# The value projection of a stick-breaking attention as seven block products instead of eight

## The chip, the core and the metric

The kernel runs on one core of one Trainium2 chip. The metric is device time in microseconds for one execution of the whole program. All matrix products are made in three passes of a 32-bit format with a reduced mantissa: each operand is split into a high part and a low part (what is left), and high x high, high x low and low x high are summed. The engines are TensorE (PE: matmuls; PEld: its weight loads), VectorE (DVE), ScalarE (ACT), GpSimd (POOL) and the queue of SyncE (SP) that issues nearly all DMAs.

## The reference

Two layers on 512 tokens of width 1024: a pooling mixer with an MLP, then an attention with an MLP. Cut to what matters here:

```python
def stick_breaking_attention(q, k, v):            # 16 heads of 64, blocks of 128 queries
    z = einsum('bhqd,bhkd->bhqk', q_blk, k_blk) / 8
    log1m = where(mask, -softplus(z), 0.0)        # mask: key strictly before query
    excl = cumsum(log1m, reverse=True) - log1m
    a = where(mask, exp(log_sigmoid(z) + excl), 0.0)
    out = einsum('bhqk,bhkd->bhqd', a, v_blk)

def sq_relu_mlp(h, w_up, w_down):
    return matmul(square(relu(matmul(h, w_up))), w_down)

# layer 0: x += norm(pool_mixer(norm(x)));  x += norm(mlp(norm(x)))
kv = matmul(rms_norm(x, kv_norm_g), w_kv)         # (512 x 1024) @ (1024 x 2048): keys and values
# layer 1: q = norm(x) @ w_q;  x += norm(attention(q, k, v) @ w_o);  x += norm(mlp(norm(x)))
```

The value projection is the second half of that product: 512 x 1024 tokens by 1024 x 1024 weights.

## The kernel before

**Planner.** The program is written as a sequence of tile operations. A planner then fixes the order on each engine ahead of time: what stands first in the program goes first among the operations that it holds to be ready. Inside regions marked `manual_schedule` TensorE keeps the written order, and `issue_after(x)` keeps an operation behind `x` on its engine. A tile with `bufs=n` has n buffers under its tag, and the next use waits until one is released.

**First MLP (`mlp(0, ...)`, about 35 to 350 us of the span).** The up projection makes 32 blocks of 128 hidden units (`up` and `up_block`, L672 to 674). The down projection takes 28 of them in five groups through the class `Seven`, which already multiplies 2x2 blocks by seven products (L560), with combinations on VectorE (L514, L533), splits on ScalarE and VectorE (L272, L273) and sums into `y` on VectorE (L569). The last four hidden blocks go through `contract` plainly (`dn` weights, L310 to 312).

In 27 of the 35 steps of this MLP `split_apart` prepares weights of the attention beside it: load 512 KB, scale by the norm's gain on ScalarE (L144; eight calls on 128 columns for keys and queries, four on 256 for values), cast the high part on ScalarE (L219), subtract on VectorE (L220), and store both parts to device memory (`kept`, L175). All 24 of the attention's value, key and query weights go this way.

**Weights in time.** `queue` lists the weights in the order in which they will be used. `get` takes one; `fill` fetches ahead until four (`ahead`) are made and not yet used. `make` reloads a kept weight as two DMAs (L230). A weight that is not kept goes through `weight()`: load into `raw` (two buffers, L123), scale on ScalarE, cast on ScalarE (L133), subtract on VectorE (L135). Both ways need a buffer of `place`: three under the tag `w` and one under `wx`, so four weights in all. At the seam to the attention the first four entries of the attention's queue stand ahead of the MLP's last `dn` weights.

**Attention.** The order of work is `ATT_ORDER`, a list of short words:

- V: `values(u, tiles)`, four heads' values for some token tiles; 24 matmuls of 256 columns a tile (`mm3`, L310 to 312), copied out on ScalarE (L910).
- K: the first half of a key block (tokens 0 and 1). J: keys of a head pair. Q: its queries. Each is 24 matmuls of 512 columns or the same in halves (L672 to 674); ScalarE casts (L944, L945, L960) and VectorE subtracts (L946, L961).
- N: transpose a token tile into `xnh`, `xnl` (L383; split at L272, L273).
- S: the scores of a pair (L994), then for both heads sigmoids (L1019, L1023), a scan (L1025) and a product (L1029).
- T: transpose one head's weights (L1042), copied out by ScalarE (L1044). A: mix the values (L1053).
- O: a part of the output projection. E: its last part, with the norms.
- W: `split_here`, one step of preparing the eight output weights and four up weights of the second MLP. Each step stores one, splits one (L185, L186) and loads one (L194), into a buffer of `grow`, `spare` or, for two of four, `raw`.

The program runs all operations of a pair in that order: S of one pair, then J and Q of the next, then T and A of the first. With `V0` the value work stands spread over the pairs, a few token tiles at a time. The token tiles 2 and 3 come out of the first MLP's closing norms only after the attention has begun (N2, N3).

Of the kernel before, what the change touches and what calls it, by code (L numbers as in the profile page):

```python
# [55 lines left out]
    (w[0], int(w[1:2] or 0), [int(c) for c in w[2:]])  # L56
    for w in """V00 W K0 V01 N2 V02 N3 V03 J0 Q0 W V10 V11 S0 W J1 Q1 T00 T01 V13 S1 V12 A0 J2 W T10 W Q2 W W T11 A1
    S2 O00 O03 O01 J3 T21 Q3 O02 T20 S3 J4 A2 Q4 W V20 T30 S4 V21 W W J5 T31 Q5 A3 T40 W V23 T41
    V22 S5 A4 W J6 Q6 T51 T50 V30 S6 A5 J7 Q7 T60 T61 V31 S7 W W V33 V32 A6 O10 O11 T70 T71
    O12 A7 O13 E2""".split()  # L60
]


# [8 lines left out]
def trunk(ctx, tc, x, consts, gcol, grow, pw, wup, wdn, wq, wk, wv, wo, out):  # L72
# [80 lines left out]
    def place(k):  # L153
# [3 lines left out]
        if k == ("o", 6):  # L157
            both = att_pool[0].tile([P, 2, D], F32R, tag="v", bufs=2, name=name("w"))
# [18 lines left out]
    def split_here():  # L177
# [9 lines left out]
        if here:  # L187
# [7 lines left out]
            going.append([k, 0, raw, None])  # L195

    def split_apart(mp):
        if going and going[0][1] == 3:
            k, _, raw, hi, _ = going.pop(0)
            keep_parts(k, hi, raw)  # L200
        if apart:
            k, src, scaled = apart.pop(0)
            n = len(apart) % 5
            if n < 3:
                raw = mp.tile([P, D], F32, tag="apart", bufs=3, name=name("apart"))
            else:
                raw = spare_tile() if n == 3 else work.tile([P, D], F32, tag="grow", name=name("apart"))

            with tc.issue_after(latest["sp"].ins) if "sp" in latest else nullcontext():
                nc.sync.dma_start(raw, src)  # L210
            going.append([k, 0, raw, None, scaled])
        for x in going:
            k, n, raw, hi, scaled = x
            if n == 1:
                if scaled is not None:
                    scaled(raw)
            elif n == 2:
                hi = x[3] = apart_hi[0][:, len(kept) % 2]
# [27 lines left out]
    for l in range(2):  # L246
        if l == 1:
            n = len(queue)
            for what, i, part in ATT_ORDER:
                if what == "V" and 0 in part:  # L250
                    for h in range(2):
                        want(("v", i, h), wv[i, h], gains(C_KV * KC + 4 * h, 4))
                elif what == "J":
# [317 lines left out]
    def mlp(l, mp, update):  # L571
# [56 lines left out]
        for g, group in enumerate(groups):  # L628
# [6 lines left out]
            for i in range(7):  # L635
# [12 lines left out]
                else:  # L648
# [4 lines left out]
                    elif i == 5:  # L653
                        piece = lambda tag, k, bufs=1: mp.tile([P, k, D], F32R, tag=tag, bufs=bufs, name=name("dn"))
                        w, e, x = piece("w1", 3), piece("e", 1), piece("w", 3, 2)
                        c, d = (piece("apart", 1, 3)[:, 0] for _ in range(2))
                        dn_pool[0] = [[w[:, 0], w[:, 1]], [w[:, 2], e[:, 0]], [c, d], [x[:, 0], x[:, 1]]]
# [235 lines left out]
    with tc.tile_pool(name="att", bufs=1, reuse_waits="tile") as ap:  # L893
        att_pool[0] = ap

        def values(u, part):
            if u not in vs:
                w = [get(("v", u, h)) for h in range(2)]
                vs[u] = w, ap.tile([P, T, 4, HD], F32, tag="v", bufs=2, name=name("v"))
            w, v = vs[u]  # L900
            for s in part:
                need(s)
                pv = ps()
                for k in range(KC):
                    c = slice((k % 4) * 256, (k % 4) * 256 + 256)
                    mm3(
                        pv[:, :256], xnh[:, k, TS[s]], xnl[:, k, TS[s]],
                        in_turn(w[k // 4][0][:, c], 256), in_turn(w[k // 4][1][:, c], 256), k == 0, k == KC - 1,
                    )
                nc.scalar.copy(v[:, s].rearrange("p h d -> p (h d)"), pv[:, :256])  # L910

# [120 lines left out]
        def transposed(w):  # L1032
            parts = {}
            for tiles in ((0,), (1, 3), (2,)):
                pt = ps()
                c = 0
                turned = ap.tile([P, S], F32, tag="at", bufs=8, name=name("at"))
                for s in tiles:
# [8 lines left out]
        def mix_pair(p):  # L1047
            po, v = ps(), vs[p // 2][1]
            with tc.manual_schedule(engines={mybir.EngineType.PE}):
                for s in range(T):  # L1050
                    for a in range(2):
                        turned, c = parts[p, a][s]
                        nc.tensor.matmul(  # L1053
                            po[half[a], s * P :], v[:, s, (2 * p + a) % 4], turned[:, c : c + S - s * P],
                            start=s == 0, stop=s == T - 1, skip_group_check=True,
                        )
            if p < PAIRS - 1:
                both = ap.tile([P, D], F32R, tag="ohl", bufs=5, name=name("ohl"))
            else:
# [3 lines left out]

        vs, os, wos, y = {}, {}, {}, y_tiles()

# [11 lines left out]
        for what, i, part in ATT_ORDER:  # L1077
            if what == "V":
                values(i, part)
            elif what == "W":  # L1080
# [95 lines left out]
```

## Time and profile before

| | |
|---|---|
| median of 3 runs | 909.21 us (908.27 to 909.58) |
| the profiled execution | 909.54 us |
| its span in the profile | 907.7 us |
| granted TensorE clock | 0.998 |
| PE busy | 896.7 us (99%), 4762 matmuls |
| DVE busy | 663.4 us (73%) |
| ACT busy | 553.4 us (61%) |
| POOL busy | 92.0 us (10%) |
| DMA | 169.35 MB, mean 187 GB/s |

The profile is one execution. Its stage rows give busy time of each engine in a stretch of the span. The busy time of one matmul overlaps that of the next, so the distance between starts is what a matmul takes in a stream. Rows that group instructions read: line, engine, operation, output from input, shape, count, busy us, mean ns, then the idle time just before and what ended it.

### The profile page before, as it was taken

To read this page: it belongs to the slowest core of one execution; us is meant where nothing else is said; L and a number is where in the kernel's file an instruction comes from. 1 tells how busy PE (TensorE), PEld (TensorE's weight loads), DVE (VectorE), ACT (ScalarE), POOL (GpSimd) and SP (SyncE) were. 2 spreads that over 40 slices of the span, in tenths; PEclk is the share of its full clock that TensorE was granted. 3 is DMA by queue.
4 is the path that set the end of the run, shared out by engine and by line. 5 is a ranking of instruction groups with operands and counts; after the bars stand their busy time and mean duration, and the time that the engine had idled before them with its cause. 6 is when DMAs were issued, how large, how long until landed. Compare 5 with 4: busy or idle time off the path is not lost.

```text
span 907.7 us, 12363 instructions
## 1 busy us (share of the span) xinstructions
PE 896.7 (99%) x4762; PEld 783.4 (86%) x4762; DVE 663.4 (73%) x682; ACT 553.4 (61%) x956; POOL 92.0 (10%) x86
## 2 busy tenths in 40 slices
PE   9999999999999999999999999999999999999996
PEld 7998888888888888987888887898888888888886
DVE  5966798997988966476463664965596876968956
ACT  6668989797884638576656652456554454544632
POOL 2100000000000014000000000402130310303103
PEclk9999999999999999999999999999999999999999
DMA  7444989698693423999624355332504233133102
GB/s 286 144 185 137 350 295 336 265 327 334 220 352 142 162 93 117 365 414 333 238 110 168 149 196 184 139 129 86 205 23 164 92 139 117 46 140 116 47 24 92
DMA packets 46928, 169.35 MB, mean 187 GB/s; under 512 B 4832, under 2 KB 5306, under 8 KB 46870
## 3 DMA queue, kind: packets, MB, share of 16 engines
q1 hardware_dynamic: 46722, 168.55, 50.7%
q8 instruction: 37, 0.61, 0.3%
q14 instruction: 21, 0.17, 0.1%
q10 hardware_dynamic: 148, 0.02, 0.0%
HBM read 128.71 MB, written 39.85 MB: 186 GB/s over the span
## 4 chain that ended last, share of the span: by engine, by line
PE 91%; DMA 2%; DVE 2%; ACT 2%; issue 1%; POOL 1%; SPq 0%; POOLq 0%; DVEq 0%; ACTq 0%
PE ps L560 27%; PE ps L672 14%; PE ps L674 14%; PE ps L673 14%; PE ps L310 4%; PE ps L311 4%; PE ps L312 4%; PE ps L1053 2%; PE ps L1042 2%; PE ps L994 2%; PE ps L811 2%; DMA kept<-xn 1%; DMA xn<-in_wdn 1%; PE ps L787 1%; DVE x L357 1%
## 5 line engine op out<-in xcount | busy, mean ns | idle before, releaser
L560 PE MATMUL ps<-w,a 128*128 128x512 f32 x1176 | 267.1, 379 | 0.2 <-DVE a L273 0.2
L673 PE MATMUL ps<-xnl,w 128*128 128x512 f32 (+1 forms) x712 | 254.8, 358 | 0.6 <-DVE xnl L273 0.6
L672 PE MATMUL ps<-xnh,w 128*128 128x512 f32 (+1 forms) x712 | 254.9, 360 | 0.0
L674 PE MATMUL ps<-xnh,w 128*128 128x512 f32 (+1 forms) x712 | 254.7, 358 | 0.0
L560 PEld LDWEIGHTS ps<-w,a 128*128 128x128 f32 x1176 | 222.0, 189 | 32.4 <-DVE a L273 0.6
L673 PEld LDWEIGHTS ps<-xnl,w 128*128 128x128 f32 x712 | 135.0, 190 | 15.9 <-DVE xnl L273 1.0
L674 PEld LDWEIGHTS ps<-xnh,w 128*128 128x128 f32 x712 | 134.9, 190 | 16.0 <-issue 0.8
L672 PEld LDWEIGHTS ps<-xnh,w 128*128 128x128 f32 x712 | 134.3, 190 | 15.8 <-issue 0.5
L135 DVE TENSOR_TENSOR w<-raw,w 128x1024 fp32r<-128x1024 f32 x56 | 70.9, 1268 | 51.3 <-ACT w L133 51.3
L569 DVE TENSOR_TENSOR y<-ps,y 128x512 f32<-128x512 f32 x124 | 83.4, 683 | 26.2 <-PE ps L560 26.2
L133 ACT CAST w<-raw 128x1024 fp32r<-128x1024 f32 x56 | 58.4, 1044 | 69.1 <-PE ps L674 68.3
L345 POOL TENSOR_TENSOR y<-y,grow 128x512 f32<-128x512 f32 x12 | 18.8, 1568 | 550.3 <-ACT xn L276 550.3
L1025 DVE TENSOR_TENSOR_SCAN e<-u,begin 128x1280 f32<-128x1280 f32 x16 | 45.2, 2825 | 34.7 <-ACT u L1019 33.8
L272 ACT CAST w<-e 128x1536 fp32r<-128x1536 f32 (+1 forms) x30 | 41.7, 1390 | 40.3 <-DVE e L533 31.0
L272 ACT CAST a<-r 128x768 fp32r<-128x768 f32 (+1 forms) x60 | 47.0, 785 | 29.2 <-DVE r L514 17.7
L273 DVE TENSOR_TENSOR w<-e,w 128x1536 fp32r<-128x1536 f32 (+1 forms) x30 | 54.8, 1825 | 9.1 <-ACT w L272 8.9
L273 DVE TENSOR_TENSOR a<-r,a 128x768 fp32r<-128x768 f32 (+1 forms) x60 | 59.1, 985 | 0.0
L144 ACT ACTIVATE apart<-apart,gc 128x128 f32<-128x128 f32 (+1 forms) x136 | 43.7, 401 | 0.1
L273 DVE TENSOR_TENSOR w<-xn,w 128x1536 fp32r<-128x1536 f32 (+1 forms) x20 | 33.0, 1652 | 11.0 <-ACT w L272 10.6
L273 DVE TENSOR_TENSOR w<-w,w 128x1536 fp32r<-128x1536 f32 (+1 forms) x20 | 34.6, 1728 | 8.1 <-ACT w L272 8.1
L276 ACT ACTIVATE xn<-y 128x512 f32<-128x512 f32 (+1 forms) x24 | 14.9, 622 | 41.4 <-DVE y L418 41.4
L272 ACT CAST w<-xn 128x1536 fp32r<-128x1536 f32 (+1 forms) x20 | 27.8, 1390 | 19.4 <-PE ps L560 19.4
(145 smaller groups left out, 1345.2 us busy)
## 6 DMA issues: line engine op xcount, KB each, us to landing
w<-kept SPq DMA_DIRECT2D x70, 512.0 KB, 4.9
raw<-in_wup SPq DMA_DIRECT2D x62, 512.0 KB, 4.2
w<-in_wdn SPq DMA_DIRECT2D x8, 1536.0 KB, 6.7
kept<-wx SPq DMA_DIRECT2D x24, 512.0 KB, 6.2
xn<-in_wdn SPq DMA_DIRECT2D x8, 1536.0 KB, 6.6
kept<-apart SPq DMA_DIRECT2D x22, 512.0 KB, 4.9
kept<-xn SPq DMA_DIRECT2D x12, 512.0 KB, 8.1
kept<-spare SPq DMA_DIRECT2D x8, 512.0 KB, 5.5
```

The lines of the kernel that those rows point to most:

```text
L133: nc.scalar.copy(hi, raw)
L135: nc.vector.tensor_tensor(out=lo, in0=raw, in1=hi.bitcast(F32), op=ALU.subtract)
L144: nc.scalar.mul(c, c, gc[:, lo + k : lo + k + 1])
L272: latest["act"] = nc.scalar.copy(hi, src)
L273: latest["dve"] = nc.vector.tensor_tensor(out=lo, in0=src, in1=hi.bitcast(F32), op=ALU.subtract)
L310: nc.tensor.matmul(dst, ah, bh, start=start, stop=False)
L560: nc.tensor.matmul(bank, a[:, x, q, TS[t]], by_twos(w[:, z, q], NS[0]), start=start and q == 0 and k == 0, stop=q == self.n - 1 and k == 2 ...
L569: nc.vector.tensor_tensor(out=part, in0=bank, in1=part, op=ALU.add)
L672: nc.tensor.matmul(pu[:, cols], wh[:, k, :], xh, start=k == 0, stop=False)
L673: nc.tensor.matmul(pu[:, cols], wh[:, k, :], xl, start=False, stop=False)
L674: nc.tensor.matmul(pu[:, cols], wl[:, k, :], xh, start=False, stop=k == KC - 1)
L1025: nc.vector.tensor_tensor_scan(out=e[:, ::-1], data0=u[:, 1:][:, ::-1], data1=begin[:, ::-1], initial=0.0, op0=ALU.mult, op1=ALU.max,)
```

## The change

The value projection is made as C = X W with X and W cut into 2x2 blocks: two halves of the tokens (256 each) by two halves of the width, and two halves of the width by two halves of the heads. Seven products of such blocks replace eight. Each product is two token tiles by 512 columns: 4 x 3 matmuls of 512 columns a tile.

- Three products use weight blocks as they are (W11, W21, W22; `VALUES` 0, 5 and 6). They are no longer kept: `weight()` makes them in the attention, with two scalings each a half.
- Four use combined weight blocks. `value_forms` makes them in the first MLP in 27 steps: it loads and scales the four blocks of each half, combines them with four VectorE operations, splits and stores the results.
- From step 16 on, `split_apart` prepares keys and queries of pairs 0 to 3. Those of pairs 4 to 7 are no longer prepared there; `weight()` makes them in the attention.
- Four products use combined token blocks. `form` (F) makes the combinations on VectorE from the high and low parts and splits them.
- `value_product` (V) runs a product; products 0, 2, 4 and 6 add into the same two PSUM banks one after the other. Each result is copied by ScalarE or added by VectorE into `v_all`, which holds all heads.
- All seven products stand before pair 2 in the new `ATT_ORDER`. The W steps begin after A0, two to a pair.
- Buffers: `at` has 6 instead of 8, `ohl` 6 instead of 5; the tile of output weight 6 lies on the scan's operands.

```diff
 ATT_ORDER
-    V00 W K0 V01 N2 V02 N3 V03 J0 Q0 W V10 V11 S0 W J1 Q1 T00 T01 V13 S1 V12 A0 J2 W T10 W Q2 W W T11 A1
-    S2 O00 O03 O01 J3 T21 Q3 O02 T20 S3 J4 A2 Q4 W V20 T30 S4 V21 W W J5 T31 Q5 A3 T40 W V23 T41
-    V22 S5 A4 W J6 Q6 T51 T50 V30 S6 A5 J7 Q7 T60 T61 V31 S7 W W V33 V32 A6 O10 O11 T70 T71
-    O12 A7 O13 E2
+    V5 K0 N2 N3 F3 V3 J0 Q0 F2 S0 V1 J1 Q1 F1 V0 T00 T01 V2 F4 V4 S1 V6 A0 W J2 W Q2 T10 T11 S2 A1 W W J3 Q3
+    T20 T21 O00 S3 O01 A2 W W J4 O02 Q4 O03 T30 T31 S4 A3 W W J5 Q5 T40 T41 S5 A4 W W J6 Q6 T50 T51 S6 A5 W W J7 Q7
+    T60 T61 S7 W W A6 O10 O11 O12 T70 T71 O13 A7 E2
+VALUES = (
+    (0, "11", (0, 0)), (1, "s3", None), (2, "s2", None), (3, "22", None), (4, "s1", None),
+    (5, "12", (1, 0)), (6, "s4", (1, 1)),
+)
+    def value_forms():            # per half h, one entry a step, from step 8 * h on
+            listed = [
+                [(load, "B"), (load, "D")],
+                [(scale, "B"), (scale, "D"), (load, "A")],
+                [(make_form, "E", "D", "B", minus), (scale, "A")],
+                [(make_form, "B", "B", "A", minus)],
+                [(parts_of, "B"), (load, "C")],
+                [(store, "B", 4), (make_form, "G", "E", "A", plus), (scale, "C")],
+                [(parts_of, "E")],
+                [(store, "E", 1), (make_form, "C", "C", "G", minus)],
+                [(parts_of, "G")],
+                [(store, "G", 2), (parts_of, "C")],
+                [(store, "C", 3)],
+            ]
 def split_apart(mp):
-        if apart:
+        for job, *rest in form_steps[n]:
+            job(*rest)
+        if apart and n >= 16:
...
-            apart.extend(x for x in queue[n:] if x[0][0] != "o")
+            apart.extend(x for x in queue[n:] if x[0][0] in "kq" and x[0][1] < 4)
...
+        def form(i):
+            if i == 3:
+                s, z = sums[3], other = quarter(), quarter()
+                on(out=s, in0=high["11"], in1=high["21"], op=ALU.subtract)
+                on(out=z, in0=low["11"], in1=low["21"], op=ALU.subtract)
+                on(out=s, in0=s, in1=z, op=ALU.add)
+            elif i == 2:          # five such operations: 21 + 22, then minus 11
+            elif i == 1:
+                s = sums[1]
+            else:                 # two operations: 12 minus the sum of F2
+            hi, lo = (quarter().bitcast(F32R) for _ in range(2))
+            split(s, hi, lo)
+        def value_product(i):
+            key = VALUES[i][1]
+            w = [get(("v", i, h)) for h in range(2)]
+            for t in range(2):
...
+                for q in range(4):
+                    cols = NS[q % 2]
+                    for n, (x, z) in enumerate(((0, 0), (0, 1), (1, 0))):
+                        nc.tensor.matmul(
+                            bank, a[x][q], in_turn(w[q // 2][z][:, cols], 512),
+                            start=(i == 0 or not linked) and q == 0 and n == 0, stop=q == 3 and n == 2,
+                        )
+                if i == 1:
+                    to(1, 1, False)
+                    to(1, 0, True)
+                else:
+                    to(*{0: (0, 0, True), 2: (1, 0, True), 3: (1, 0, False), 4: (1, 1, True),
+                         5: (0, 0, False), 6: (0, 1, False)}[i])
+            fill()
```

More of the change, by code (lines that the diff above doesn't have):

```diff
@@ L157, in place @@
         if k == ("o", 6):
-            both = att_pool[0].tile([P, 2, D], F32R, tag="v", bufs=2, name=name("w"))
+            return [
+                att_pool[0].tile([P, NSEG + 1 + 55 * a], F32R, tag=f"u{a}", name=name("w"))[:, :D] for a in range(2)
+            ]
         elif k == ("o", 7):
@@ L195, in split_here, with load, scale, make_form @@
             going.append([k, 0, raw, None])
-    def split_apart(mp):
+    def value_forms():
+        steps = [[] for _ in range(27)]
+        for h in range(2):
+            names = "B0 D3 A1 E2 C4 G3".split() if h == 0 else "B0 D1 A2 E3 C4 G1".split()
+            spot = {x[0]: int(x[1]) for x in names}
+            source = {"A": (0, 0), "B": (0, 1), "C": (1, 0), "D": (1, 1)}
+            got = {}
+            def load(x, h=h, got=got, spot=spot):
+                t = got[x] = buffer(spot[x])
+                with tc.issue_after(latest["sp"].ins) if "sp" in latest else nullcontext():
+                    nc.sync.dma_start(t, wv[source[x]][h])
+            def scale(x, h=h, got=got):
+                gains(C_KV * KC + 4 * source[x][0] + 2 * h, 2)(got[x])
+            def make_form(out, x, y, op, got=got, spot=spot):
+                if out not in got:
+                    got[out] = buffer(spot[out])
+                nc.vector.tensor_tensor(out=got[out], in0=got[x], in1=got[y], op=op)
+            def parts_of(x, got=got):
+                hi = apart_hi[0][:, len(kept) % 2]
+                raw = got[x]
+                nc.scalar.copy(hi, raw)
+                nc.vector.tensor_tensor(out=raw, in0=raw, in1=hi.bitcast(F32), op=ALU.subtract)
+                got[x] = raw, hi
+            def store(x, i, h=h, got=got):
+                raw, hi = got[x]
+                keep_parts(("v", i, h), hi, raw)
+            minus, plus = ALU.subtract, ALU.add
+            listed = [
[10 more added lines that the diff above has]
+                [(store, "C", 3)],
+            ]
+            for n, jobs in enumerate(listed):
+                steps[8 * h + n].extend(jobs)
+        return steps
@@ new lines, in buffer @@
+    def buffer(n):
+        if n < 3:
+            return apart_raw[0][:, n]
+        return spare_tile() if n == 3 else work.tile([P, D], F32, tag="grow", name=name("apart"))
+    form_steps, apart_raw = [], [None]
+    def split_apart(mp):
+        if not form_steps:
+            form_steps.extend(value_forms())
+            apart_raw[0] = mp.tile([P, 3, D], F32, tag="apart", name=name("apart"))
+        n = split_apart.n = getattr(split_apart, "n", -1) + 1
+        for job, *rest in form_steps[n]:
+            job(*rest)
@@ L200, in split_apart @@
             keep_parts(k, hi, raw)
-        if apart:
+        if apart and n >= 16:
             k, src, scaled = apart.pop(0)
[L203 to L209, printed above, removed]
+            raw = buffer((0, 2, 1, 3, 4)[(n - 16) % 5])
+            with tc.issue_after(latest["sp"].ins):
                 nc.sync.dma_start(raw, src)
@@ L212, in split_apart @@
         for x in going:
[L213 to L217, printed above, removed]
+            k, m, raw, hi, scaled = x
+            if m == 1:
+                scaled(raw)
+            elif m == 2:
                 hi = x[3] = apart_hi[0][:, len(kept) % 2]
@@ L655, in mlp @@
                         w, e, x = piece("w1", 3), piece("e", 1), piece("w", 3, 2)
-                        c, d = (piece("apart", 1, 3)[:, 0] for _ in range(2))
+                        both = piece("apart", 3)
+                        c, d = both[:, 0], both[:, 1]
                         dn_pool[0] = [[w[:, 0], w[:, 1]], [w[:, 2], e[:, 0]], [c, d], [x[:, 0], x[:, 1]]]
@@ L894, in trunk @@
         att_pool[0] = ap
[L896 to L910, printed above, removed]
+        v_all = ap.tile([P, T, HEADS, HD], F32, tag="v", name="v")
@@ L1047, in mix_pair @@
         def mix_pair(p):
[L1048 removed]
+            po = ps()
             with tc.manual_schedule(engines={mybir.EngineType.PE}):
@@ L1057, in mix_pair @@
             if p < PAIRS - 1:
-                both = ap.tile([P, D], F32R, tag="ohl", bufs=5, name=name("ohl"))
+                both = ap.tile([P, D], F32R, tag="ohl", bufs=6, name=name("ohl"))
             else:
@@ L1078, in trunk @@
             if what == "V":
-                values(i, part)
+                value_product(i)
+            elif what == "F":
+                form(i)
             elif what == "W":
```

62 lines of the change are left out of this document (53 added, 9 removed).

## The prediction

> **What bounds the kernel now.** I read the page first (engine shares, then the chain that ended last), then busy time by stage, then single matmuls in order of time.
>
> ```profile
> span 907.7 us, 12363 instructions
> PE 896.7 (99%) x4762; PEld 783.4 (86%) x4762; DVE 663.4 (73%) x682; ACT 553.4 (61%) x956; POOL 92.0 (10%) x86
> PE 91%; DMA 2%; DVE 2%; ACT 2%; issue 1%; POOL 1%; SPq 0%; POOLq 0%; DVEq 0%; ACTq 0%
> 96.00:330.00 234.00, 233.83 (x1083) 204.22 (x1082) 204.64 (x197) 180.01 (x300) 0.00 (x0) 1.00 0.74 269
> 350.00:362.00 12.00, 11.19 (x94) 10.77 (x93) 7.04 (x13) 8.95 (x21) 5.50 (x19) 1.00 0.62 219
> 388.00:560.00 172.00, 171.40 (x1052) 143.66 (x1051) 99.88 (x79) 99.30 (x220) 0.00 (x0) 1.00 0.59 219
> ```
>
> TensorE is busy for 99% of the span and is 91% of the chain. The stage rows (PE, PEld, DVE, ACT, POOL busy, granted clock, DMA share, GB/s) are the first MLP, the seam into the attention, and most of the attention. TensorE loses 0.2, 0.8 and 0.6 us there. In the attention VectorE and ScalarE are only 58% busy: that slack is what the change spends. The profiled run took 909.54 us, 1.8 above its span and 0.3 above the median of 909.21. The sum is made against 909.54.
>
> **The change part by part.** First the matmuls of the value projection.
>
> ```profile
> L310 PE MATMUL ps<-w,xnh 128*128 128x256 f32 x128 | 35.7, 281 | 0.8 <-ACT xnh L272 0.8
> L311 PE MATMUL ps<-w,xnh 128*128 128x256 f32 x128 | 35.2, 276 | 0.3 <-DMA w<-kept 0.3
> L312 PE MATMUL ps<-w,xnl 128*128 128x256 f32 x128 | 35.2, 276 | 0.0
> ```
> ```profile
> 351.44 0.27 PE L310 MATMUL ps<-w,xnh 128*128 128x256 f32 x1
> 354.12 0.28 PE L672 MATMUL ps<-xnh,w 128*128 128x256 f32 x1
> 659.83 0.38 PE L674 MATMUL ps<-xnh,w 128*128 128x512 f32 x1
> 662.42 0.38 PE L674 MATMUL ps<-xnh,w 128*128 128x512 f32 x1
> ```
>
> Durations overlap, so starts give the price. From 351.44 to 354.12 are 24 matmuls of 256 columns: 0.1117 each. From 659.83 to 662.42 are 12 of 512: 0.2158 each. Removed: 4 units x 4 token tiles x 24 = 384, 42.9 us. Added: 7 products x 2 tiles x 4 blocks x 3 = 168 of 512 columns, 36.3 us. **TensorE: -6.6 us.** [...]
>
> The first MLP. Of 24 weights split there, 16 remain (8 combined blocks, 4 keys, 4 queries), and VectorE forms 8 combined blocks.
>
> ```profile
> L220 DVE TENSOR_TENSOR apart<-apart,wx 128x1024 f32<-128x1024 f32 x18 | 21.9, 1217 | 0.0
> 159.06 2.44 ACT L144 ACTIVATE apart<-apart,gc 128x128 f32<-128x128 f32 x8
> 161.40 1.03 ACT L133 CAST w<-raw 128x1024 fp32r<-128x1024 f32 x1
> 162.34 0.58 ACT L592 ACTIVATE r<-ps 128x512 f32<-128x512 f32 x1
> ```
>
> VectorE: 24 subtractions become 16 plus 8 forms of the same size, never more than one a step: 0 net. ScalarE loses eight times 2.34 + 0.94 (starts above), more with the wider scalings. Stores and reloads fall from 24 MB each to 16. TensorE waited 0.2 us here, so I take 0. If the covering slack went, one 1.2 us form could appear; bounds -0.2 to +2.
>
> The token forms: 10 VectorE operations and 4 splits, 14 x 1.22 = 17, plus 8 evacuations that add. They lie behind J0, Q0, S0 and the other products, in a stretch where VectorE is about half busy: 0, upper bound 3, nothing below.
>
> **The seam.** Before, TensorE bridges the wait for token tiles 2 and 3 with three blocks of 24 (V00, K0, V01).
>
> ```profile
> 359.48 1.04 PE L383 MATMUL ps<-ident,xn 128*128 128x128 f32 x8
> 361.32 0.38 PE L310 MATMUL ps<-w,xnh 128*128 128x256 f32 x1 [0.81 <-ACT xnh L272]
> w<-kept SPq DMA_DIRECT2D x70, 512.0 KB, 4.9
> w<-kept SPq DMA_DIRECT2D x22, 512.0 KB, 7.7
> ```
>
> They end when the transposes start at 359.48. Now V5 (24 x 0.2158 = 5.2 us) ends at 356.6. K0 should follow, but the four weights fetched ahead are V5's and V3's halves. The key weight needs the buffer of V5's first half, free after 18 of 24 matmuls, at 355.3. At 4.9 us (page) or 7.7 (between 350 and 440 us) it lands at 360.2 to 363. V3 needs tile 2. So TensorE idles from 356.6 to 359.48: **+2.9 us**; what comes next is as late as before. Bounds: +1.3 (a landing in 2.6) and +5.5 (K0 stays ahead of V3 in TensorE's order and lands at 363).
>
> **The loop over head pairs.** This is the largest term. Eight key and query weights (pairs 4 to 7) are no longer prepared in the first MLP but in the attention, as are six value weights; and the value products no longer stand between later pairs.
>
> ```profile
> 509.21 2.18 PE ps L1042 x20
> 514.08 2.15 PE ps L994 x16
> 516.22 2.31 PE ps L1053 x16
> ```
>
> A pair without filler is J and Q (48 x 0.2158 = 10.4), T 2.18, S 2.15, A 2.31: 17.0 us of TensorE.
>
> ```profile
> L944 ACT CAST k<-ps 64x512 fp32r<-64x512 f32 x16 | 9.3, 580 | 34.5 <-PE ps L674 21.0 <-DVE kl L946 13.4
> L945 ACT CAST k<-ps 64x512 fp32r<-64x512 f32 x16 | 9.3, 580 | 0.2
> L960 ACT CAST q<-ps 64x512 fp32r<-64x512 f32 x16 | 9.3, 580 | 11.3 <-PE ps L674 7.5 <-DVE q L961 3.7
> 509.79 1.33 ACT L1044 COPY at<-ps 128x512 f32<-128x512 f32 x3
> 511.75 1.35 ACT L1044 COPY at<-ps 128x512 f32<-128x512 f32 x3
> 515.20 0.60 ACT L1019 ACTIVATE u<-ps 128x511 f32<-128x511 f32 x1 [0.71 <-PE ps L994]
> 520.18 0.75 ACT L272 CAST ohl<-ps 128x512 fp32r<-128x512 f32 x1
> L185 ACT CAST xn<-raw 128x1024 fp32r<-128x1024 f32 x6 | 6.7, 1113 | 4.7 <-DMA kept<-xn 4.7
> ```
>
> ScalarE per pair: sigmoids 5.0 (515.20 to 520.18), copies of the transposed weights 2.7, casts 27.9/8 = 3.5, the cast of the mixed heads 0.6: 11.8. New: two weights at 3.28 (scaling plus cast) = 6.6, and the two W steps now written into every pair, 2 x 1.05 = 2.1. That is 20.4 against 17.0.
>
> ```profile
> L1025 DVE TENSOR_TENSOR_SCAN e<-u,begin 128x1280 f32<-128x1280 f32 x16 | 45.2, 2825 | 34.7 <-ACT u L1019 33.8
> L1029 DVE TENSOR_TENSOR w<-w,e 128x1280 f32<-128x1280 f32 x16 | 23.8, 1490 | 3.5 <-ACT w L1023 2.1
> L961 DVE TENSOR_TENSOR q<-ps,q 64x512 fp32r<-64x512 f32 x16 | 11.0, 689 | 15.3 <-ACT q L960 15.2
> L946 DVE TENSOR_TENSOR kl<-ps,k 64x512 fp32r<-64x512 f32 x16 | 11.0, 688 | 13.1 <-ACT k L945 13.0
> L135 DVE TENSOR_TENSOR w<-raw,w 128x1024 fp32r<-128x1024 f32 x20 | 24.3, 1218 | 6.8 <-ACT w L133 6.8
> DMA to landing us min/median/max: 2.6/5.6/11.3
> ```
>
> VectorE per pair: (45.2 + 23.8 + 11.0 + 11.0)/8 = 11.4, the mixed heads 0.7, two weights and two W steps 4 x 1.22 = 4.9: 17.0 of 17.0. Both engines have lost their slack.
>
> Can the work move earlier? Only two raw buffers exist. Pair 5's weights hold both until the buffers of the first output weights come free after O03, so pairs 6 and 7 cannot be scaled sooner. From O03 to the end of Q7 TensorE has three pairs, 51 us. ScalarE must do 3 x 11.8, two casts of pair 5 (1.9), four whole weights (13.1) and about four W steps (4.2): 54.6. That is 3.6 short even if packed without a hole. The rows above show the holes: ScalarE waited 13.4 + 3.7 us for VectorE between casts, 2.1 a pair. I charge some 0.8 of these for each of three pairs, the rest being filled with scalings: 2.4. **Loop: +6.0 us.** Bounds: 0, if the four W steps run before (54.6 - 4.2 is under 51), and +13.6, if all four late pairs run at 20.4. I take the middle, as the shortage is small beside the stage.
>
> DMA carries less in all; SP's order changes: a raw load queued behind a store that waits for a split comes late, included in the upper bound. After a load lands (5.6 us), scaling, cast and subtraction still take 4.5, so pair 7's keys, whose raw buffers W7 and W8 use first, are the likeliest to be late.
>
> Sum: 909.5 - 6.6 + 2.9 + 6.0 = **911.8 us**.
>
> **The rivals.** (1) Faster. W steps and scalings fit the holes, since a planner fixes the order ahead: in the first MLP it keeps TensorE at 99.9% with VectorE at 87% and ScalarE at 77%.
>
> ```profile
> 318.42 9.81 SPq L194 DMA_DIRECT2D raw<-in_wo x2
> ```
>
> This row speaks for it: the first two output weights are loaded 33 us ahead of the attention, so W steps do run early. Against it: ScalarE would be near 100% for 50 us, not 77%. The loop term goes to 0: 909.5 - 6.6 + 2.9 = 905.8, and 904.2 with the seam at its lower bound. It decides from loop stalls below 1.6 us.
> (2) ScalarE sets the pace of all four late pairs: +13.6 instead of 6.0, 919.4. For it: 20.4 against 17.0; against it: O02 and O03 lengthen pair 4, and buffers let weights be made ahead.
> (3) The seam is long enough to cost clock too: if the granted clock halved for a stretch as long as the gap, +1.5 more, 913.3. The stage rows show 1.00 throughout, but no idle time over 0.8 us. [...]
> (4) The change gives TensorE nothing, because the 512-column operand is read at twice the stride: 909.5 + 8.9 = 918.4. The 512-column rows of the MLPs, read alike, speak against it.
>
> **How the numbers follow.** Forecast 0.45 (its own range 908 to 916), rival 1 0.34, rival 2 0.14, rival 3 0.04, rival 4 0.03. A measurement here tells about 0.2%, 1.8 us, from no change: faster is below 907.4, slower above 911.0. Faster: rival 1 and the lower edge of the forecast, 0.36. Same: 0.18, the forecast with a loop term of 1.6 to 5.2. Slower: 0.46. The range 903.5 to 919 runs from rival 1 with the seam's lower bound to rival 2 and leaves out 2 in 10.
>
> **What would show it.** Right: 168 value matmuls at 0.216; a gap of some 3 us ahead of token tile 2's transposes; TensorE waiting in pairs 5 to 7 for key or query weights, or in the transposes for the scan's product, with ScalarE over 90% busy there; no new wait in the first MLP. Wrong: TensorE 99% busy from pair 4 to pair 7 (rival 1), or waits inside the value products for forms or weights, which I price at nothing.

## The result: 935.9 us, slower by 2.9%, and the profile after

| | before | after |
|---|---|---|
| median | 909.39 us (908.27 to 909.59) | 935.94 us (931.79 to 937.40, 4 runs) |
| ratio after/before | | 1.0287, 95% interval 1.0251 to 1.0323 |
| profiled execution | 909.54 us | 937.04 us |

The direction was the likeliest of the three that were forecast. The size, 911.8 in a range of 903.5 to 919, was not. Single executions of the changed kernel lie up to 4 us from its median, so a difference of a few us between single runs below is only a hint; there the gaps in the traces decide.

In the changed kernel L742 to L744 are the matmuls of keys and queries, L1024 those of the value products, L1127 the scores, L1175 the transposes, L1186 the mix; L1093 and L1094 cast and subtract the queries; L192 and L193 do so in a W step; L149, L138 and L140 scale, cast and subtract a weight made in the attention. The page first: span, busy times, granted clock by slice, and the chain that ended last.

```profile
span 935.3 us, 11909 instructions
PE 902.6 (97%) x4546; PEld 778.9 (83%) x4546; DVE 700.7 (75%) x718; ACT 566.7 (61%) x954; POOL 93.0 (10%) x86
PEclk9999999999999999899999879999999999999999
PE 77%; ACT 10%; DVE 6%; DMA 4%; issue 3%; POOL 0%; DVEq 0%; POOLq 0%; SPq 0%; ACTq 0%
```

TensorE has 216 matmuls fewer and yet 5.9 us more of busy time. The clock row points to the reason: three slices stand at 0.8, 0.8 and 0.7 of full clock. ScalarE and VectorE now hold 16% of the chain instead of 4%. The stage rows (busy time of PE, PEld, DVE, ACT, POOL, then granted clock, DMA share, GB/s):

```profile
96.00:330.00 234.00, 233.78 (x1083) 204.30 (x1083) 206.82 (x199) 160.92 (x232) 0.00 (x0) 1.00 0.60 216
350.00:362.00 12.00, 9.12 (x43) 7.96 (x42) 5.14 (x11) 7.68 (x17) 4.79 (x19) 0.88 0.63 221
362.00:388.00 26.00, 20.88 (x118) 18.55 (x117) 22.51 (x23) 13.24 (x22) 0.00 (x0) 0.89 0.86 311
480.00:510.00 30.00, 29.27 (x154) 24.08 (x153) 17.42 (x14) 28.67 (x70) 0.00 (x0) 1.00 0.15 53
510.00:540.00 30.00, 23.85 (x124) 18.62 (x122) 21.17 (x18) 21.35 (x49) 0.00 (x0) 0.89 0.60 214
540.00:570.00 30.00, 25.73 (x130) 19.59 (x132) 18.09 (x16) 19.28 (x42) 0.00 (x0) 0.83 0.62 225
```

The first MLP lost nothing (233.78 of 234, before 233.83). The seam has lost 2.9 us of PE (before, 0.8) and some clock (0.88; before, 1.00). Behind it, from 362 to 388, VectorE is busy for 22.51 of 26 us; before, it was 14.41:

```profile
362.00:388.00 26.00, 25.65 (x184) 23.86 (x183) 14.41 (x14) 16.30 (x32) 0.00 (x0) 1.00 0.93 355
```

Pair 4 (480 to 510) still runs, with ScalarE busy for 28.67 of 30 us. Then PE falls to 124 and 130 matmuls in 30 us, at a clock of 0.89 and 0.83. In these two rows, where TensorE waits, neither helper is full: ScalarE is busy for 21.35 and 19.28 of 30 us, VectorE for 21.17 and 18.09. What TensorE waited for (total, times, longest):

```profile
PE ps L1127 <- DVE q L1094: 11.0, 3, 5.1
PE ps L1175 <- DVE w L1162: 3.5, 3, 1.3
PE ps L742 <- DMA w<-kept: 2.9, 1, 2.9
PE ps L1024 <- DVE v L1033: 2.2, 1, 2.2
PE ps L1127 <- ACT at L1177: 1.9, 2, 1.2
```

The scores wait 11 us for the subtraction of the queries on VectorE. One line is the predicted seam: K0 waits 2.9 us for its kept weight. The first of the three long waits, S0 (TensorE, then VectorE, then the load and the cast of the W step that stands ahead):

```profile
378.31 0.38 PE L744 MATMUL ps<-xnh,w 128*128 128x512 f32 x1
383.81 1.44 PE L1127 MATMUL ps<-k,q 128*128 128x512 f32 x4 [5.12 <-DVE q L1094]
386.54 3.61 PE L1024 MATMUL ps<-w,s 128*128 128x512 f32 x8
378.97 1.23 DVE L990 TENSOR_TENSOR s<-s,xnl 128x1024 f32<-128x1024 f32 x1
381.81 1.23 DVE L193 TENSOR_TENSOR apart<-apart,xn 128x1024 f32<-128x1024 f32 x1 [1.62 <-ACT xn L192]
383.07 0.68 DVE L1094 TENSOR_TENSOR q<-ps,q 64x512 fp32r<-64x512 f32 x1
375.08 0.33 SPq L201 DMA_DIRECT2D apart<-in_wo  x1
380.74 1.04 ACT L192 CAST xn<-apart 128x1024 fp32r<-128x1024 f32 x1 [2.53 <-issue]
```

Q0's last matmul starts at 378.31, but the subtraction of its result only at 383.07: VectorE keeps a fixed order, and a W step's split stands ahead, which itself waits for its cast on ScalarE. The row of that cast names no releaser for ScalarE's 2.53 us of idle time, but its semaphore does: the load issued at 375.08 landed 5.6 us later, at 380.67, and the cast started at once. So the wait begins with a late load at the head of a fixed order. After the wait, eight matmuls of 512 columns take 3.61 us, most of them 0.43 apart instead of 0.216: half clock. The second long wait, in pair 5 (VectorE, then ScalarE), has much the same form:

```profile
514.56 1.22 DVE L193 TENSOR_TENSOR raw<-raw,xn 128x1024 f32<-128x1024 f32 x1
515.70 0.68 DVE L1079 TENSOR_TENSOR kl<-ps,k 64x512 fp32r<-64x512 f32 x1
516.89 1.23 DVE L193 TENSOR_TENSOR spare<-spare,xn 128x1024 f32<-128x1024 f32 x1 [0.52 <-ACT xn L192]
518.15 0.69 DVE L1094 TENSOR_TENSOR q<-ps,q 64x512 fp32r<-64x512 f32 x1
515.81 1.04 ACT L192 CAST xn<-spare 128x1024 fp32r<-128x1024 f32 x1 [5.56 <-DVE raw L193]
516.76 0.57 ACT L1093 CAST q<-ps 64x512 fp32r<-64x512 f32 x1
```

ScalarE's W cast waits 5.56 us for VectorE, the queries' cast is queued behind it, and their subtraction stands behind one more W split. The records of the clock in the trace, with the idle gaps of TensorE just ahead (each as the whole distance between two starts, of which 0.1 to 0.2 is normal):

```
half clock from (us, length)   idle gaps ahead of it (start, us)
359.13  3.41                   356.2  3.26   K0, kept weight
383.03  6.83                   378.3  5.50   S0, query subtraction
427.40  3.41                   424.7  2.60   V6, sum into v on VectorE
519.56  6.83                   513.7  1.10; 515.8  3.18   T and S of pair 5
543.45 10.24                   539.6  1.60; 542.2  3.28   T and S of pair 6
```

A sixth stretch, at 932.6, belongs to the end of the program; the kernel before has one there too (904.1).

The books: 27.5 us more, although the matmuls should save 6.6, so 34.1 were lost. The gaps of the table with 1.22 at 496.3, 1.65 at 519.0, 1.44 at 521.3 and 1.59 at 580.3 make 26.4, or some 25 us without the normal distances. The rest, some 9 us, is the price of the half clock by subtraction. The starts of the matmuls inside the five stretches, 30.7 us in all, say the same: added up, they lie some 9 us further apart than at full clock.

### The profile page after: what moved, and what is told of

Read it like the earlier page. It is cut to its first block, busy times and chain, and to the rows that moved or that the text cites. A ratio compares the mean times of both kernels' runs of the same rounds, so it can differ in the third digit from the quotient of the medians.

```text
span 935.3 us, 11909 instructions
## 1 busy us (share of the span) xinstructions
PE 902.6 (97%) x4546; PEld 778.9 (83%) x4546; DVE 700.7 (75%) x718; ACT 566.7 (61%) x954; POOL 93.0 (10%) x86
## 4 chain that ended last, share of the span: by engine, by line
PE 77%; ACT 10%; DVE 6%; DMA 4%; issue 3%; POOL 0%; DVEq 0%; POOLq 0%; SPq 0%; ACTq 0%
PE ps L629 24%; PE ps L742 12%; PE ps L743 12%; PE ps L744 12%; PE ps L1024 3%; PE ps L379 2%; PE ps L381 2%; PE ps L380 2%; ACT raw L149 2%; PE ps L881 2%; ACT apart L149 1%; PE ps L1127 1%; PE ps L1186 1%; DMA xn<-in_wdn 1%; ACT w L138 1%
## 5 line engine op out<-in xcount | busy, mean ns | idle before, releaser
L742 PE MATMUL ps<-xnh,w 128*128 128x512 f32 (+1 forms) x712 | 254.6, 360 | 2.9 <-DMA w<-kept 2.9
L744 PE MATMUL ps<-xnh,w 128*128 128x512 f32 (+1 forms) x712 | 254.5, 358 | 0.0
L742 PEld LDWEIGHTS ps<-xnh,w 128*128 128x128 f32 x712 | 134.4, 190 | 19.1 <-DMA w<-kept 3.3
L744 PEld LDWEIGHTS ps<-xnh,w 128*128 128x128 f32 x712 | 135.0, 190 | 15.3
L140 DVE TENSOR_TENSOR w<-raw,w 128x1024 fp32r<-128x1024 f32 x70 | 88.2, 1261 | 59.8 <-ACT w L138 59.7
L138 ACT CAST w<-raw 128x1024 fp32r<-128x1024 f32 x70 | 73.5, 1052 | 82.8 <-PE ps L744 81.1
L341 ACT CAST a<-r 128x768 fp32r<-128x768 f32 (+1 forms) x60 | 47.0, 785 | 26.4 <-POOL r L583 11.7
L1158 DVE TENSOR_TENSOR_SCAN e<-u,begin 128x1280 f32<-128x1280 f32 x16 | 45.2, 2824 | 20.6 <-ACT u L1152 20.1
L149 ACT ACTIVATE raw<-raw,gc 128x128 f32<-128x128 f32 (+1 forms) x76 | 28.9, 518 | 16.6 <-DMA raw<-in_wv 13.6
L661 ACT ACTIVATE r<-ps 128x512 f32<-128x512 f32 x56 | 33.1, 591 | 8.6 <-PE ps L744 8.6
```

The source lines that it names most:

```text
L138: nc.scalar.copy(hi, raw)
L140: nc.vector.tensor_tensor(out=lo, in0=raw, in1=hi.bitcast(F32), op=ALU.subtract)
L149: nc.scalar.mul(c, c, gc[:, lo + k : lo + k + 1])
L341: latest["act"] = nc.scalar.copy(hi, src)
L661: nc.scalar.activation(split_up(r, 256), in_order(pu, 256), ACT.Relu)
L742: nc.tensor.matmul(pu[:, cols], wh[:, k, :], xh, start=k == 0, stop=False)
```

## Experiments

The theories: (A) the loss is idle gaps, made by the fixed order on VectorE and ScalarE, and the half clock after each; (B) the work moved into the attention is too much for the two engines wherever it stands; in the last run (C) the late weights lack buffers. The texts on the runs without late weights and without W steps use A and B in another sense: there A means that the late weights overload the two engines, B that the W steps stand in front.

**The seam.** K0's weight stands among the first four:

```diff
+            queue.insert(n + 2, queue.pop(n + 4))
             queue[n - GRP : n + GRP] = queue[n : n + GRP] + queue[n - GRP : n]
```

> The first key weight is fetched among the first four, before the second half of V3's weights; nothing else changes. If the gap before K0 (3.3 us) and the half clock after it come from that late weight, the gap goes, the clock stays at 1.0 until the scores of pair 0, and the time falls by 3 to 5 us, to 932 to 934. Rival: the wait only moves to the transposes of token tile 2, and the time stays within 1.5 us of 937.

Measured 930.76 us, just below the expected 932 to 934. The gap ahead of K0 and the half clock at 359 are gone; S0's gap stays (3.88) and so do the late pairs. The half clock behind V6 went too, though its gap is still 2.49.

**Does the gap cost clock?** Fourteen matmuls whose result nothing reads stand behind V5, so that TensorE has work in the gap:

```diff
             fill()
+            if i == 5:
+                with tc.issue_after(last.ins):
+                    for n in range(14):
+                        nc.tensor.matmul(spare_bank, xnh[:, 4, TS[0]], in_turn(other[:, NS[n % 2]], 512), ...)
```

> Fourteen useless matmuls (3.0 us, into a bank that nobody reads) stand behind V5, in the gap before K0; all else as changed. If idle time of TensorE is what halves the clock, the half-clock stretch of 3.4 us that begins at 359 us is gone, and the others (383, 427, 519, 543 us) stay; the time falls by about 1.5 us at most. Rival: the clock falls for another reason (power, the kind of work), and the stretch at 359 stays.

Measured 933.06. TensorE's order of time and the stage row of this kernel:

```profile
356.15 3.19 PE L1048 MATMUL ps<-w,xnh 128*128 128x512 f32 x14
359.82 0.35 PE L742 MATMUL ps<-xnh,w 128*128 128x256 f32 x1 [0.48 <-DMA w<-kept]
350.00:362.00 12.00, 11.36 (x60) 9.65 (x59) 5.27 (x12) 8.08 (x19) 4.54 (x18) 1.00 0.65 238
```

K0 starts no earlier (359.82 against 359.47), but the clock of this stage is 1.00 instead of 0.88. So in this stage the half clock came with the idle gap, not with the place in the program. Against the expectation the stretch behind V6 is gone here as well, with a gap of 2.49 left (see the last section).

**What the parts cost.** Late key and query weights left out (pairs 4 to 7 use the parts of pairs 0 to 3), their scaling alone left out, the W steps left out (in the changed kernel and in the kernel before), the token forms left out (the products then use single token blocks), and all of these together. Parts of the edits:

```diff
+        if k[0] in "kq" and k[1] >= 4:            # late weights
+            kept[k] = kept[k[0], k[1] - 4]
...
-    want(("k", i), wk[i], gains(C_KV * KC, KC))    # scaling; the same for q
+    want(("k", i), wk[i], gains(C_KV * KC, KC) if i < 4 else None)
...
     def split_here():                              # W steps
+        if here:
+            kept[here.pop(0)[0]] = kept["k", 0]
+        return
...
-                form(i)                            # forms
+                pass
```

> The key and query weights of pairs 4 to 7 are replaced by the kept parts of pairs 0 to 3, so their scaling, cast and subtraction in the attention are left out. Theory A (ScalarE and VectorE carry too much in the late pairs because of these eight weights): the gaps of pairs 5 and 6 and the half clock after them go, 937 falls to 919 to 924. Theory B (the W steps, queued in front of what TensorE waits for, are the cause): the gaps stay, less than 5 us is gained.

> The change with the scaling of the eight late key and query weights left out (64 calls, 8 x 2.34 us of ScalarE); their loads, casts and subtractions stay. If ScalarE's load is what counts, most of the 18.5 us of the run a_kq is gained, 920 to 924. If VectorE's order or the two raw buffers count, less than a third is, 930 or more.

> The twelve W steps are left out; the output weights and four up weights are replaced by a kept key weight. Theory A: less than 5 us is gained, the gaps of pairs 5 and 6 stay. Theory B: these gaps go, 937 falls to 919 to 924. If both this and the run without the eight splittings gain some 15 us, neither alone is the cause: the sum overfills the two engines, and either one relieves it.

> The kernel before with its twelve W steps left out. If that work was hidden before, it gains under 2 us (908 to 910), and the 15 us that the same edit gained in the changed kernel are the change's doing. Rival: W steps cost in both, and this one gains 5 us or more.

> The run a_seam (930.8) with the token combinations left out; products use single token blocks. If the gap at S0 (3.9 us) and its 6.8 us of half clock are VectorE's ten combinations and four splits in front of the query's subtraction, the gap is below 1 us and 5 to 8 us are gained: 923 to 926. Rival: S0 waits because the queries themselves are late, 929 or more.

> Left out together: the late key weight, the splitting of eight key and query weights and of six value weights, the W steps, and the token combinations (products use single token blocks). What is left is the change in the matmuls alone, at 168 instead of 384. If the matmul term of -6.6 us is right and all the loss sits in these parts, 903 to 905 at clock 1.0. If 907 or more, the products themselves cost more than was priced (their evacuations, or the two banks they hold).

| left out | us | against the kernel that it is cut from |
|---|---|---|
| late k and q weights | 918.50 | -17.4 (935.94) |
| only their scaling | 925.92 | -10.0 |
| W steps | 922.13 | -13.8 |
| W steps, kernel before | 907.73 | -1.6 (909.31 beside it) |
| forms (seam mended) | 927.00 | -3.8 (930.76) |
| all, with mended seam and kept value weights | 902.03 | -33.9 |

Each is a single run; without scaling the time lies between the two forecasts. The last kernel is 8.5 below the kernel before on the same chip (910.51), with W steps worth 1.6 there: the seven products themselves give 6.9, predicted 6.6, with an error of 1 to 2 us (the kernel before alone took 908.3 to 911.0 in all its runs). Its page shows why it can:

```profile
span 900.2 us, 11694 instructions
PE 888.8 (99%) x4546; PEld 772.1 (86%) x4546; DVE 652.8 (73%) x678; ACT 512.5 (57%) x848; POOL 90.5 (10%) x86
```

The other rows do not add: with 5.2 for the seam they make 40.2, so they relieve in part the same waits. In the kernel before the W steps were hidden (1.6); on top of the late weights they cost 13.8. The forms' 3.8 is within the scatter of single runs, but in the trace S0's gap falls from 3.88 to 1.77 without them, and its half clock goes.

The late pairs are measured by the scores' own row (first and last start): changed kernel, then without late weights, without W steps, without scaling.

```profile
L1127 PE MATMUL ps<-k,q x32: 220/363/793, 496.3 to 569.0; 128*128 128x512 f32 x8, 128*128 128x384 f32 x8, 128*128 128x256 f32 x8, 128*128 128x128 f32 x8
L1129 PE MATMUL ps<-k,q x32: 220/311/505, 494.9 to 550.1; 128*128 128x512 f32 x8, 128*128 128x384 f32 x8, 128*128 128x256 f32 x8, 128*128 128x128 f32 x8
L1130 PE MATMUL ps<-k,q x32: 220/338/797, 488.6 to 554.0; 128*128 128x512 f32 x8, 128*128 128x384 f32 x8, 128*128 128x256 f32 x8, 128*128 128x128 f32 x8
L1127 PE MATMUL ps<-k,q x32: 220/338/795, 494.5 to 557.8; 128*128 128x512 f32 x8, 128*128 128x384 f32 x8, 128*128 128x256 f32 x8, 128*128 128x128 f32 x8
```

From pair 4's first to pair 7's last are 72.7, 55.2, 65.4 and 63.3 us. The span is three pairs and one S. With the prediction's rows ScalarE has 20.4, 13.8, 18.3 and 15.8 us of work a pair (less 6.6, 2.1, and twice 2.3 for the scaling); TensorE has 17.0, 53 us in all. So the late pairs lose 19.7 us; without the late weights 17.5 of these go, without the W steps 7.3. The rest of the W steps' price lies ahead of pair 4, whose scores start 7.7 us earlier without them. Without scaling ScalarE has less than TensorE, and 10 us are still lost: ScalarE's sum alone does not explain the loss.

**Other orders.** If only the order matters, there should be a whole kernel at 909 or less. The forms 3 and 2 written later (seam mended):

```diff
-V5 K0 N2 N3 F3 V3 J0 Q0 F2 S0 V1 J1 Q1 F1 V0 ... V4 S1 V6 A0 W
+V5 K0 N2 N3 V3 J0 Q0 S0 F3 F2 V1 J1 Q1 F1 V0 ... V4 S1 A0 V6 W
```

> The first key weight early as in the run a_seam, and the token combinations F3 and F2 written behind S0 instead of ahead of it, A0 between V4 and V6. If VectorE's combinations in front of the query's subtraction cause the 3.9 us gap at S0, it shrinks below 1 us with its half-clock stretch, and the gap before V6 (2.5 us) shrinks too: 930.8 falls to 922 to 925. Rival: the planner places the combinations there anyway, 929 to 932.

Measured 930.52: no difference to the mended seam. The planner still puts the forms ahead of the queries' subtraction. What is written later is not issued later where the planner is free.

More weights in the first MLP: its steps run from 0 to 32, and 13 of the 16 keys and queries are prepared there. In the first of two runs the W steps stand before pair 4; in the second the forms are held behind the latest VectorE operation, with J1 between S0 and V1 and J2 between A0 and V6.

```diff
-            apart.extend(x for x in queue[n:] if x[0][0] in "kq" and x[0][1] < 4)
+            apart.extend(x for x in queue[n:] if x[0][0] in "kq")
+            del apart[13:]
-        steps = [n for n in range(1, 28)] if l == 0 else []
+        steps = list(range(33)) if l == 0 else []
+                with tc.issue_after(latest["dve"].ins):     # second run, in form()
+                    nc.vector.tensor_tensor(**kw)
```

> A whole kernel: a_flate's two edits, the W steps spread over the value products and pairs 0 to 3, and 13 instead of 8 key and query weights kept in the first MLP (its steps run on to the last but two). If the loss is overfilled ScalarE and VectorE in pairs 4 to 7 plus the early gaps, 903 to 908, faster than before. If the first MLP's tail or the crowded value stretch cannot take the moved work, 912 to 920, with TensorE waiting there.

> A whole kernel: first key weight early, the token combinations held behind the subtraction that VectorE did last (the query's), J1 between S0 and V1, J2 between A0 and V6, and 13 instead of 8 key and query weights kept in the first MLP; the W steps stay late. If the early gaps come from VectorE's order and the late ones from the late weights, TensorE has no gap over 2 us and the time is 903 to 909. Rival: gaps move to the new neighbours (V1 waiting for its combination, V0 for its raw weights), 912 to 922.

Measured 929.71 and 925.73, above all forecasts. Waits of TensorE in the second:

```profile
PE ps L1029 <- ACT w L138: 8.4, 1, 8.4
PE ps L631 <- ACT a L343: 2.7, 1, 2.7
```

The late gaps shrink, but value product 0 now waits 8.4 us for its raw weight's cast, and the longer preparation opens a gap late in the first MLP, which had none. Next, with value product 0 ahead of 1 and eleven weights prepared in the first MLP. (The recorded text says that the parts come from earlier pairs and that data differ. That is wrong: they are the right weights, prepared in four more steps of the first MLP.)

```diff
+V5 K0 N2 N3 V3 J0 Q0 F3 S0 J1 V0 F2 V1 Q1 F1 T00 T01 V2 F4 V4 S1 A0 J2 V6 W Q2 W ...
-            here.extend((("up", 1, j), wup[1, j], None) for j in range(4))     # second and third
```

> The changed kernel with the seam mended (K0's weight among the first four), value product 0 ahead of product 1, the token forms written behind the subtractions of queries on VectorE, and eleven of the sixteen late key and query parts taken from earlier pairs' kept parts instead of being prepared in the loop (the data of those pairs is then that of other pairs). Theory A (the loss is idle gaps made by VectorE's and ScalarE's order, and the clock that halves after each): the 8.77 us gap of the kernel with J1 between goes, no gap over 3 us and no stretch at half clock, 906 to 912. Theory B (the moved work itself is too much wherever it stands): gaps of 3 to 6 us open at other places, two or more stretches at half clock, 918 or more.

> As the run before, but with ten W steps spread from Q1 to the output projection's third block, none in the pairs 4 to 7, and the four up weights of the second MLP no longer prepared by W steps. Theory A: pairs 4 to 7 without a gap over 1.5 us, 904 to 911, as long as the W steps between do not open gaps in pairs 0 to 3. Theory B: the gaps move to pairs 1 to 3, where the forms are, with stretches at half clock, 915 or more.

> As the run before the last, but the token forms issued where the planner puts them (ahead of the queries' subtraction on VectorE), and the four up weights not prepared by W steps. Theory A: S0 waits 3.5 to 4 us again with a stretch of 3.4 to 6.8 us at half clock there, and pairs 4 to 7 without gaps: 908 to 914. Theory B: late gaps remain, 918 or more.

Measured 926.74, 930.18 and 929.05: theory B's numbers in all three. The gap of value product 0 did go, as A said, and others took its place: in the first, 3.18 and 3.28 us ahead of the scores of pairs 5 and 6; in the second, 5.84 at S0 and 6.13 in pair 5, though no W step is left in the late pairs; in the third, 4.33 at S0. The numbers are B's, but B's cause is not shown by them: ahead of the gap of 6.13 ScalarE was not full but idle (see the last run).

**The place of the W steps**, in the otherwise unchanged text of the kernel: behind the queries, then behind the scores; and all repairs together.

```diff
-A3 W W J5 Q5 T40 T41 S5 A4
+A3 J5 Q5 W W T40 T41 S5 A4         # first, pairs 3 to 7 alike
+A3 J5 Q5 T40 T41 S5 W W A4         # second
```

> The changed kernel with nothing but the place of the W steps altered: in the pairs 3 to 7 the two W steps stand behind the pair's queries instead of ahead of its keys. Theory A (the late gaps come from the order on VectorE and ScalarE: a W split stands ahead of the subtraction that the scores wait for): the two gaps of 3.2 and 3.3 us ahead of the scores of pairs 5 and 6 fall under 2 us, at least one of the two late half-clock stretches goes, 924 to 931. Theory B (the amount of work on the two engines): the gaps stay or move to the scan's product, 933 to 940.

> The changed kernel with the two W steps of the pairs 3 to 7 moved behind that pair's scores. Theory A: the waits for the queries' subtraction go, but the two casts on ScalarE now stand ahead of the sigmoids or of the copies of the transposed weights, so that about 1 us a pair comes back at the mix or the transposes: 922 to 931. Theory B: 933 to 940.

> All the repairs that keep the computation whole, together: K0's weight among the first four, value product 0 ahead of 1, forms behind the queries' subtraction, thirteen of the sixteen key and query weights prepared in the first MLP (five more steps of it), and W steps behind the queries. Theory A: from the kernel with J1 between S0 and V1 (925.7) the 8.8 us gap of V0 and its 6.8 us at half clock go (-12), the late pairs' rest goes in part (-3): 909 to 914. Theory B: 918 or more, with gaps at new places.

Measured 946.92, 946.40 and 926.62. The first two are the slowest of all, far from theory A's numbers. But they do not test the place alone, as a row of SyncE's queue in the first shows (wait of TensorE, then loads):

```profile
PE ps L742 <- ACT w L138: 9.4, 1, 9.4
423.64 2.07 SPq L128 DMA_DIRECT2D raw<-in_wo  x2
462.83 3.99 SPq L201 DMA_DIRECT2D raw<-in_wo  x2
472.55 0.33 SPq L128 DMA_DIRECT2D raw<-in_wk  x1
```

L128 is `weight()`, L201 a W step. With the W steps so late, the first two output weights are not yet kept when they are fetched: `weight()` prepares them a second time, in all three runs. Here they hold the two raw buffers from 423.64 until their casts at 460.50 and 464.16; W steps take the buffers next, and pair 4's keys are loaded at 472.55. In the changed kernel W steps load into raw at 426.7, their stores are issued by 436.4, and that load goes at 443.8. So these runs speak neither for nor against theory A. They do show the chain of two buffers which the prediction described. Does it set the time of the changed kernel too? The W steps take turns on the other two buffers:

```diff
-            n = len(here) % 4
+            n = 2 + len(here) % 2
```

> The changed kernel with one alteration: the W steps take turns on the two buffers of spare and grow and never use the two raw buffers, which are left to the late weights. In the kernel with the W steps behind the queries J4 waited 9.6 us for a key weight whose load (at 472.6) stood behind loads of W steps into raw (from 462.8). Theory C (the late weights are late because W steps hold the raw buffers): the loads of pairs 6 and 7 into raw go 10 to 20 us earlier, the gaps ahead of the scores of pairs 5 and 6 fall under 1.5 us and their half-clock stretches go: 920 to 928. Theory B (the casts, scalings and subtractions themselves stand ahead of what TensorE waits for, whenever they are loaded): the scalings only move forward by a pair, the gaps stay or move to pairs 3 to 5, 933 to 942.

Measured 934.59 (four runs, 930.80 to 936.92; ratio to before 1.0271, 1.0236 to 1.0306): no difference to the changed kernel. The row of its scores:

```profile
L1127 PE MATMUL ps<-k,q x32: 220/337/796, 498.5 to 565.0; 128*128 128x512 f32 x8, 128*128 128x384 f32 x8, 128*128 128x256 f32 x8, 128*128 128x128 f32 x8
```

66.5 instead of 72.7: pair 6 has lost its gap, but pair 5's has grown to 5.94, and the gap of V6 to 2.98. Three runs have this gap of some 6 us in pair 5: the one without W steps (5.96), the second of the three with value product 0 ahead (6.13) and this one. In the same order, what ScalarE did ahead of the keys' second cast there:

```profile
508.05 0.40 ACT L149 ACTIVATE raw<-raw,gc 128x128 f32<-128x128 f32 x1 [4.16 <-DMA raw<-in_wq]
513.55 0.40 ACT L149 ACTIVATE raw<-raw,gc 128x128 f32<-128x128 f32 x1 [4.31 <-DMA raw<-in_wq]
517.96 0.40 ACT L149 ACTIVATE raw<-raw,gc 128x128 f32<-128x128 f32 x1 [4.14 <-DMA raw<-in_wq]
```

The scaling of a query weight stands ahead of the cast, and ScalarE is idle for more than 4 us until that weight has landed. In the last run its load was issued at 514.73, just after a subtraction that ended at 514.71 had freed a raw buffer. So this gap needs no W step in the raw buffers: as far as the trace shows, two of them are too few there for the late weights alone. A third was not tried.

Of the whole kernels none comes under the kernel before; the best, 925.73, is 14.8 above it. Theory B, taken as engines that are full, does not fit the late rows of the changed kernel; theory A is not shown either, as no order came near 909. What stays open is whether a better order of all queues, or more buffers, could. In these runs the late gaps went, without new ones elsewhere, only where work was left out.

## Why the prediction was wrong

- **TensorE, -6.6: right.** With the added work left out, the products gave 6.9, within the error of single runs. V5's 24 matmuls start 0.216 apart, as was priced.
- **First MLP, 0: right**, 233.78 of 234 us busy.
- **Seam, +2.9: right in place and cause** (2.88 us of waiting for the kept weight). That the figure is met is partly luck: the forecast ended the gap with the transposes of token tile 2 at 359.48 and had K0's weight land at 360.2 or later. It landed at 359.47, and K0 went first. What the step lacked was the clock: half speed for 3.41 us follows, which the dummy matmuls took away.
- **Token forms and value products, priced at nothing: wrong.** The argument was that VectorE is half busy there. It was before (14.41 of 26 us); with the forms it is busy for 22.51 of 26. S0 waits 5.1 us and V6 2.2 us for VectorE. Average slack is no cover for an operation queued ahead of the one that TensorE waits for. Leaving the forms out took S0's gap from 3.88 to 1.77 in the kernel with the seam mended; leaving the W steps out took it from 5.50 to 2.79.
- **Loop, +6.0, upper bound +13.6: the term that failed most.** The late pairs lost 19.7 us, and leaving out the late weights gave 17.4 of the whole time, both above the bound. The step that failed is the pooling of the helpers' time: a shortage of 3.6 us of ScalarE over three pairs, and 2.4 for holes. ScalarE was over 90% busy in pair 4 (28.67 of 30), where TensorE still ran; in pairs 5 and 6, where TensorE waited and the forecast had ScalarE over 90% busy, it was busy for 21.35 and 19.28 of 30. The time went in holes: 5.56 us of ScalarE waiting for VectorE in pair 5, with the queries' cast queued behind. The upper bound also held no clock: 17.1 us at half speed in these pairs cost at most 8.5 us. A pair took 23.4 us ((72.7 less some 2.4 for the last scores)/3), or 20.6 without that upper price of the clock. How much of the holes is order and how much buffers stays open.
- **Rival 3, the clock, chance 0.04: the idle gap at the seam did cost clock, and the chance was far too small.** It was tied to the seam alone, at +1.5, while every other idle time of the sum ran at full clock. Behind the seam's gap of 3.26 us came 3.41 us of half clock. It happened in five places and took some 9 us: single gaps of 3.26, 5.50 and 2.60 us stood ahead of it, and in pairs 5 and 6 gaps of 1.10 and 3.18, and of 1.60 and 3.28 us.
- Rival 2 (ScalarE sets the pace, 919.4) had the nearest number, and 20.4 us a pair is close to the 20.6 above. But ScalarE was not full there, and without scaling, with 15.8 us of its work a pair, 10 us were still lost: the nearness is no proof of the mechanism. Rival 4 is refuted by the first point.

## What to carry to other kernels

Work moved beside a bound engine is not paid by the helpers' mean slack: look up, in each helper's fixed order, what stands just ahead of the operation that the bound engine waits for, and price that wait. Where two helpers both come near the bound engine's pace, look for what can hold the head of each queue (the other helper, or a load that waits for a buffer): the sum of their work does not hold these holes. Price an idle gap of TensorE twice, once as idle time and once as the half clock that may follow it: in the changed kernel 3.41 us of it came behind gaps of 2.60 and 3.26 us, and 6.83 us behind one of 5.50.

## What the runs showed of the hardware

In the changed kernel half clock was recorded in five stretches (the table) of 3.41, 6.83 and 10.24 us: once, twice and three times the shortest. Their starts lie 23.89, 44.37, 92.16 and 23.89 us apart, 7, 13, 27 and 7 times the shortest. What these lengths and distances come from was not shown.

The length of a gap alone did not decide. V6's gap of the changed kernel was followed by half clock, and nine matmuls took 3.90 us:

```profile
424.47 0.65 PE L1186 MATMUL ps<-at,v 128*64 128x256 f32 x4
427.34 3.90 PE L1024 MATMUL ps<-w,s 128*128 128x512 f32 x9 [2.22 <-DVE v L1033]
```

In the kernel with J1 between S0 and V1 a longer gap, 3.07 us at 289.3 in the first MLP, was not:

```profile
285.00:295.00 10.00, 7.30 (x34) 6.10 (x33) 10.00 (x11) 4.74 (x11) 0.00 (x0) 1.00 0.63 221
295.00:300.00 5.00, 5.00 (x25) 4.38 (x24) 3.00 (x3) 5.00 (x12) 0.00 (x0) 1.00 0.34 137
```

The clock stayed at 1.00. Nor was V6's gap of 2.49 us followed by half clock with the seam mended, or with the dummy matmuls. What decides it was not shown: no run moved a gap in time on purpose.
